# One tile for both halves of the moving operand: modulated activations regrouped into runs of 512 columns

## The chip, the cores and the metric

The kernel runs on one core of a Trainium2 chip, in one launch. The metric is the device time of that launch in microseconds (us), as the median of several runs. A profile is one further execution, recorded by the hardware profiler; its times are read below as us from the start of the recorded span.

## The reference, cut to what matters

The program is two transformer-like blocks over 256 tokens of 1024 features (x), each with a second sequence of 256 tokens (the context). All arithmetic is float32. Each block begins its layers with a normalised and modulated copy of x, and in two places also of the context:

```
h  = rmsnorm(x)   * (1 + scale)   + shift        # x, modulated
hc = rmsnorm(ctx) * (1 + scale_c) + shift_c      # context, modulated
z  = h @ w_in                                    # wide projections, several layers
pc = hc @ w_in[:, some columns]                  # the context needs only a part of them
...
x  = x + gate * swiglu(h2, w_up, w_down)         # feed-forward of the last layer; h2 modulated as above
```

`swiglu` is `(silu(a) * b) @ w_down` with `a, b = split(h2 @ w_up)`; `w_up` is 1024 x 5632 and `w_down` 2816 x 1024.

## The kernel before, in words

Features lie on the 128 partitions, tokens along the free dimension, so an activation of 1024 features is eight feature tiles of 128 x 256 (`KT` = 8, `T` = 256). Weights come from memory in pieces of 1 MB. To keep float32 accuracy with the fast matmul format, every value is split into a high and a low part: ScalarE (ACT) casts the high part, VectorE (DVE) subtracts it to get the low part (`split`, L316 to L318). A product then takes three matmuls into the same bank: high x high, high weight x low activation, low weight x high activation (`mm3`, L364 to L367). The splits of weights run all the time, in quarters of 512 columns, two pieces ahead of use.

The modulated activations live in one tile `HH`, with axes [128, part (high, low), sequence (x, context), 8 feature tiles, 258]. The last two of the 258 columns are used in one trick only (below). So for one feature tile the x columns and the context columns of the same part are each a run of 256, far apart; and so are x's high and low part. Two helpers take both runs in one matmul, as a moving operand of 2 x 256 columns:

- `cols_both` (L381) multiplies a weight column block with x and context at once. It serves the four `xb` pieces of the first layer and the four `f` pieces of the third (`lru_in`, `forget`): 128 such matmuls on each of L365, L366 and L367.
- `cols_split` (L386) serves the feed-forward (all `up` pieces but the first): high weight x (x high, x low) in one matmul of 512 columns (L394), then low weight x (x high) in one of 256 (L395). The two halves of the bank are added by ACT and DVE (L397, L398). It uses two banks in turn, and a bank must be emptied before the next piece may write it.

Everywhere else (`cols2`, `toks`) x alone is used, as runs of 256.

**The early columns.** At the start of the second layer and of the feed-forward, the first weight piece does not wait for the norm. While the residual is added, `residual` (L676 to L681) writes X scaled by `1 + scale`, high and low, into the context half of `HH` (free at that time) and `shift_columns` puts the shift into the two spare columns. `cols_early` (L630) multiplies 48 times with these 258 columns, in the order high weight x high, low weight x high, high weight x low, and then DVE multiplies the two banks with the norm (L643, out `t`), after ACT has copied one column (L642, `c`). Meanwhile ACT computes the norm (`rs`, L300), and `modulate` (L599) makes the proper activations for the later pieces: DVE `xa` (L593), ACT high part (L594), DVE low part (L595), for each of the eight feature tiles.

**What sets the order.** The start of the kernel is written out by hand. From there the tables `L0` to `L3` give the order of steps, and a scheduler places the instructions of each engine by priority and by its own estimate of times; steps in `tc.high_priority()` come first among those that are ready. Each engine executes its list in order, and waits at an instruction whose inputs are not there.

Of the kernel before, what the change touches and what calls it, by code (L numbers as in the profile page):

```python
# [9 lines left out]
F32R = mybir.dt.float32r  # L10
# [13 lines left out]
EARLY = (1, 1)  # L24
# [63 lines left out]
P = 128  # L88
D = 1024
KT = 8  # L90
T = 256
# [136 lines left out]
def build(tc, gates, wp, mp, vec, xT, cT, c2T, tok, cst, crow, out, dbg=None):  # L228
    nc = tc.nc
# [8 lines left out]
    con = pool("con")  # L238
# [7 lines left out]
    def t2(name, shape=(P, 512), dt=F32):  # L246
        return wk.tile(list(shape), dt, name=name, tag="t2", bufs=NT2)

    def t1(name, shape=(P, T), dt=F32):
        return wk.tile(list(shape), dt, name=name, tag="t1", bufs=5)  # L250

    def pair(name, dt=F32):
        return [t4(f"{name}{i}", dt=dt) for i in range(2)]


    HH = con.tile([P, 2, 2, KT, T + 2], F32R, name="hh")

    def h_parts(seq, full=False):
        return [HH[:, i, seq, :, :] if full else HH[:, i, seq, :, 0:T] for i in range(2)]

    def bank(tag, bufs):
        return psum.tile([P, 512], F32, tag=tag, bufs=bufs, name=tag)
# [11 lines left out]
    def v(name, i=0, n=1):  # L274
        o, _ = VOFF[name]
        return V[:, o + i:o + i + n]
# [58 lines left out]
    def load_ahead(n_raw, n_split):  # L335
        while len(raws) < min(npieces, taken[0] + n_raw):
            r = w_p.tile([P, 2048], F32, name="w")
            nc.sync.dma_start(r, wp[len(raws)])
            raws.append(r)
        while len(pieces) < min(npieces, taken[0] + n_split):  # L340
            i = len(pieces)
            pieces.append(halves(raws[i], SW if i > SW_FROM else 2048))
            raws[i] = None
# [8 lines left out]
    def piece(last=False):  # L352

        load_ahead(LR, LSB if last else LS)
        taken[0] += 1
        p = pieces[taken[0] - 1]
        pieces[taken[0] - 1] = None
        return p

    def cut(pc, **kw):  # L360
        (k, n), = kw.items()
        return [w.rearrange(f"p ({k} m) -> p {k} m", **kw) for w in pc]

    def mm3(o, wh, wl, xh, xl, start, stop):  # L364
        nc.tensor.matmul(o, wh, xh, start=start, stop=False)  # L365
        nc.tensor.matmul(o, wh, xl, start=False, stop=False)  # L366
        nc.tensor.matmul(o, wl, xh, start=False, stop=stop)  # L367

    def mm_w(o, w, x, at, start, stop):

        if len(w) == 1:
            nc.tensor.matmul(o, w[0][at], x[0], start=start, stop=stop)
        else:
            mm3(o, w[0][at], w[1][at], x[0], x[1], start, stop)
# [6 lines left out]
    def cols_both(o, w, j):  # L381

        for k in range(KT):
            mm_w(o, w, [HH[:, i, :, k, 0:T] for i in range(2)], np.s_[:, k, 128 * j:128 * (j + 1)], k == 0, k == KT - 1)

    def cols_split(pc, name):  # L386

        w = cut(pc, k=KT)
        o = []
        for j in range(2):  # L390
            b = mm_bank()
            c = np.s_[128 * j:128 * (j + 1)]
            for k in range(KT):
                nc.tensor.matmul(b, w[0][:, k, c], HH[:, :, 0, k, 0:T], start=k == 0, stop=False)  # L394
                nc.tensor.matmul(b[:, 0:T], w[1][:, k, c], HH[:, 0, 0, k, 0:T], start=False, stop=k == KT - 1)  # L395
            o.append(t1(name))
            nc.scalar.copy(o[j], b[:, T:512])  # L397
            nc.vector.tensor_tensor(out=o[j], in0=o[j], in1=b[:, 0:T], op=ALU.add)  # L398
        return o
# [29 lines left out]
    def small(name, n=2):  # L429
        return con.tile([P, n], F32, name=name, tag="small", bufs=4)  # L430
# [145 lines left out]
    def mod_vector(name):  # L576
        while name not in md:
            mod_chunks(1)
        return md[name]

    def scale_g(name, g, sc, i):
        a = con.tile([P, 8], F32, name=name)
        nc.vector.scalar_tensor_tensor(out=a, in0=sc[:, :, i], scalar=1.0, in1=g, op0=ALU.add, op1=ALU.mult)
        return a

    def shift_of(name, sc, i):
        a = con.tile([P, 8], F32, name=name)
        nc.vector.tensor_copy(a, sc[:, :, i])
        return a
# [22 lines left out]
    def sumsq_all(xs):  # L612

        sq = pair("xsq")
        sums = sq[0][:, 2, :]
        for i in range(2):
            nc.scalar.activation(sq[i], xs[i], AF.Square)
        for i in range(2):
            nc.vector.tensor_tensor(out=sq[i][:, 0:2, :], in0=sq[i][:, 0:2, :], in1=sq[i][:, 2:4, :], op=ALU.add)
        nc.vector.tensor_tensor(out=sq[0][:, 0:2, :], in0=sq[0][:, 0:2, :], in1=sq[1][:, 0:2, :], op=ALU.add)  # L620
        nc.vector.tensor_tensor(out=sums, in0=sq[0][:, 0, :], in1=sq[0][:, 1, :], op=ALU.add)
        return token_sums(sums)
# [7 lines left out]
    def cols_early(pc, h, rs):  # L630

        w = cut(pc, k=KT)
        banks = [acc_bank() for j in range(2)]
        for a, b in ((0, 0), (1, 0), (0, 1)):
            for j in range(2):
                for k in range(KT):
                    nc.tensor.matmul(banks[j][:, 0:T + 2], w[a][:, k, 128 * j:128 * (j + 1)], h[b][:, k, :],  # L637
                                     start=k == 0 and a + b == 0, stop=k == KT - 1 and b == 1)
        out = []
        for b in banks:  # L640
            t, c = t1("t"), small("c", 1)
            nc.scalar.copy(c, b[:, T:T + 1])  # L642
            nc.vector.tensor_tensor(out=t, in0=b[:, 0:T], in1=rs, op=ALU.mult)  # L643
            out.append((t, c))
        return out
# [67 lines left out]
    with ExitStack() as st0:  # L713
# [4 lines left out]
        nc.vector.tensor_scalar(out=b1, in0=v("mod_b", 8, 8), scalar1=1.0, scalar2=None, op0=ALU.add)  # L718
        A0 = con.tile([P, 8, 2], F32, name="A0")
        S0 = con.tile([P, 8, 2], F32, name="S0")  # L720
        hx, hc = h_parts(0), h_parts(1)
        acc = [[acc_bank() for i in range(2)] for g in range(2)]
        mod_load(0, nc.sync.dma_start)
        warm_bank[0] = mm_bank()
# [69 lines left out]
        with tc.manual_schedule(engines={mybir.EngineType.PE, mybir.EngineType.DVE, mybir.EngineType.Activation}):  # L794
            for step, s in START:
                if step == "l":
                    for _ in range(s):
                        what, i, j = next(loads)
# [291 lines left out]
                rows += 1  # L1090

        scale1, shift1 = scale_g("a1", v("norm_g", 8, 8), mod_vector("scale1"), 0), shift_of("s1", mod_vector("shift1"), 0)
        early = h_parts(1, True) if EARLY[0] else None
        if early:
            shift_columns(early, shift1)
        table("natural_log_exp_and_others")
# [5 lines left out]

    with ExitStack() as st1:
        lp = st1.enter_context(tc.tile_pool(name="l1", bufs=1))
        hx = h_parts(0)
        with tc.high_priority():
            modulate(lambda k: X[:, k, :], rs1, scale1, shift1, hx)
        mod_chunks(MB[0])
# [72 lines left out]
        def second_context():  # L1181

            c2 = pair("c2")
            for i in range(2):
                nc.gpsimd.dma_start(c2[i], c2T[:, 4 * i:4 * i + 4, :])
            c2k = lambda k: c2[k // 4][:, k % 4, :]
            ms = sumsq_all(c2)
            rsc = rstd_of(ms[:, 0:2], D, 1e-6)
            ac2 = scale_g("ac2", v("g_mix_2", 0, 8), mod_vector("scale2"), 1)
            hc = h_parts(1)  # L1190
            modulate(c2k, rsc, ac2, shift_of("sc2", mod_vector("shift2"), 1), hc)
            return hc

        for name, g, j in L1:
# [8 lines left out]
            elif name == "c2":  # L1203
                hc = second_context()
# [17 lines left out]
        with tc.high_priority():  # L1222
            rs3 = rstd_wide(ms, eps12)
        rs2 = rstd_wide(plain_sums(), eps6)
        hx = h_parts(0)
        with tc.high_priority():
            modulate(lambda k: X[:, k, :], rs3, fgA, shift_of("sx2", mod_vector("shift2"), 0), hx)
        for k in range(KT):
# [5 lines left out]
    with ExitStack() as st2:  # L1234
# [238 lines left out]
        for name, m in L2B:  # L1473
            if name in ("md", "ml"):
                mod_chunks(m, MLATE if name == "ml" else 0)
            elif name == "p":
                w = [p.rearrange("p (w k m) -> p w k m", w=2, k=4) for p in piece()]
                mt = []
                for i, (oh, ol, gate) in enumerate(((oah, oal, "ga"), (obh, obl, "gb"))):
                    b = mm_bank()  # L1480
# [13 lines left out]
        gate2 = con.tile([P, 8], F32, name="gate2h")  # L1494
        nc.vector.tensor_scalar(out=gate2, in0=mod_vector("gate2")[:, :, 0], scalar1=0.5, scalar2=None, op0=ALU.mult)
        scale3, shift3 = scale_g("a4", v("g_ffn_2", 0, 8), mod_vector("scale3"), 0), shift_of("s4", mod_vector("shift3"), 0)
        early = h_parts(1, True) if EARLY[1] else None
        if early:
            shift_columns(early, shift3)
        table("natural_log_exp_and_others")  # L1500
# [2 lines left out]
        with tc.high_priority():  # L1503
            rs4 = rstd_wide(ms, eps6)


    hx = h_parts(0)
    with tc.high_priority():
        modulate(lambda k: X[:, k, :], rs4, scale3, shift3, hx)
    acc = []  # L1510
# [1 line left out]
    for name, m in L3:  # L1512
        if name in ("md", "ml"):
            mod_chunks(m, MLATE if name == "ml" else 0)
        elif name == "up":
            q = m % 2
            if early:
                (sa, ca), (sb, cb) = cols_early(piece(), early, rs4)
                early = None
                act(sa, sa, AF.Silu, bias=ca)  # L1520
                nc.vector.scalar_tensor_tensor(out=sa, in0=sb, scalar=cb, in1=sa, op0=ALU.add, op1=ALU.mult)
            else:
                sa, sb = cols_split(piece(), "sa4")
                act(sa, sa, AF.Silu)
                nc.vector.tensor_tensor(out=sa, in0=sa, in1=sb, op=ALU.mult)
            if q == 0:
                ff[m // 2] = t2("fh", (P, 2, T), F32R), t2("fl", (P, 2, T), F32R)
            split(*(f[:, q, :] for f in ff[m // 2]), sa)
        else:
            fh, fl = ff[m]  # L1530
            if not acc:
                acc.extend(acc_bank() for i in range(4))
            mm_rows(acc, piece(), lambda k: (fh[:, k, :], fl[:, k, :]), m == 0, m == NF // 2 - 1)
# [10 lines left out]
    for m, n in ((0, 1), (1, 1), (2, 2), (4, 2), (6, 2)):  # L1544
        o = X[:, m:m + n, :]
# [23 lines left out]
```

## Time and profile before

| | us |
|---|---|
| median of 3 runs | 924.5 |
| lowest, highest | 923.91, 930.61 |
| the profiled execution | 924.76 |
| its recorded span | 923.0 |

TensorE (PE) is the engine that works through nearly all of the span; DVE and ACT follow with 73% and 58%. Matmuls overlap: the record of one lasts longer than the distance to the next. For the rate of a stretch of matmuls one therefore takes the distance from start to start.

### The profile page before, as it was taken

To read this page: it belongs to the slowest core of one execution; us is meant where nothing else is said; L and a number is where in the kernel's file an instruction comes from. 1 tells how busy PE (TensorE), PEld (TensorE's weight loads), DVE (VectorE), ACT (ScalarE), POOL (GpSimd) and SP (SyncE) were. 2 spreads that over 40 slices of the span, in tenths; PEclk is the share of its full clock that TensorE was granted. 3 is DMA by queue.
4 is the path that set the end of the run, shared out by engine and by line. 5 is a ranking of instruction groups with operands and counts; after the bars stand their busy time and mean duration, and the time that the engine had idled before them with its cause. 6 is when DMAs were issued, how large, how long until landed. Compare 5 with 4: busy or idle time off the path is not lost.

```text
span 923.0 us, 16681 instructions
## 1 busy us (share of the span) xinstructions
PE 897.4 (97%) x6782; PEld 806.8 (87%) x6782; DVE 673.8 (73%) x1283; ACT 539.6 (58%) x985; POOL 15.3 (2%) x27
## 2 busy tenths in 40 slices
PE   8999999899999989999999999999999999999996
PEld 7776787596889789999999898999999999898896
DVE  4578886968766897878874554999688977756644
ACT  3444888686765665547473335972674865645542
POOL 1000000000000000000000000000000000000000
PEclk9999999999999999999999999999999999999999
DMA  9969673254567766664741752355666467555511
GB/s 363 414 221 352 218 251 130 82 176 167 205 251 291 312 233 214 219 238 156 267 137 55 291 202 92 137 184 205 244 218 247 153 216 250 202 184 182 183 46 47
DMA packets 32173, 190.06 MB, mean 206 GB/s; under 512 B 3584, under 2 KB 8064, under 8 KB 10976
## 3 DMA queue, kind: packets, MB, share of 16 engines
q1 hardware_dynamic: 31536, 186.50, 56.7%
q0 software_dynamic: 560, 2.49, 0.7%
q8 instruction: 53, 0.87, 0.4%
q14 instruction: 24, 0.20, 0.1%
HBM read 183.28 MB, written 1.05 MB: 200 GB/s over the span
## 4 chain that ended last, share of the span: by engine, by line
PE 84%; DVE 6%; ACT 6%; DMA 2%; issue 1%; SPq 0%; POOL 0%; DVEq 0%; ACTq 0%; POOLq 0%
PE mm L365 12%; PE mm L367 12%; PE mm L366 12%; PE mm L394 9%; PE acc L366 7%; PE acc L365 7%; PE acc L367 7%; PE mm L395 4%; PE ms L545 2%; PE acc L912 2%; PE acc L790 2%; PE acc L637 1%; DMA w<-in_wp 1%; PE ms L675 1%; ACT L300 1%; ACT w L317 1%
## 5 line engine op out<-in xcount | busy, mean ns | idle before, releaser
L318 DVE TENSOR_TENSOR w<-w 128x512 fp32r<-128x512 f32 x460 | 297.9, 684 | 78.5 <-ACT w L317 74.4
L317 ACT CAST w<-w 128x512 fp32r<-128x512 f32 x460 | 256.0, 618 | 103.1 <-PE mm L366 20.6
L367 PE MATMUL mm<-hh,w 128*128 128x256 f32 (+1 forms) x784 | 237.3, 303 | 2.9 <-DVE w L318 2.9
L365 PE MATMUL mm<-hh,w 128*128 128x256 f32 (+1 forms) x784 | 238.3, 304 | 1.0 <-ACT w L317 1.0
L366 PE MATMUL mm<-hh,w 128*128 128x256 f32 (+1 forms) x784 | 236.0, 301 | 0.0
L365 PEld LDWEIGHTS mm<-hh,w 128*128 128x128 f32 x784 | 148.8, 190 | 14.4 <-issue 5.5
L367 PEld LDWEIGHTS mm<-hh,w 128*128 128x128 f32 x784 | 148.5, 189 | 9.8 <-DVE w L318 3.5
L366 PEld LDWEIGHTS mm<-hh,w 128*128 128x128 f32 x784 | 148.8, 190 | 7.2 <-issue 1.5
L394 PE MATMUL mm<-hh,w 128*128 128x512 f32 x336 | 118.8, 397 | 0.0
L395 PE MATMUL mm<-hh,w 128*128 128x256 f32 x336 | 94.2, 281 | 0.0
L394 PEld LDWEIGHTS mm<-hh,w 128*128 128x128 f32 x336 | 63.2, 188 | 14.7
L504 DVE SCALAR_TENSOR_TENSOR w<-w,crow 128x1024 f32<-128x1024 f32 x40 | 47.7, 1219 | 22.1 <-DMA w<-in_mp 22.0
L395 PEld LDWEIGHTS mm<-hh,w 128*128 128x128 f32 x336 | 63.8, 190 | 0.1
L366 PE MATMUL acc<-fl,w 128*128 128x256 f32 x176 | 49.7, 283 | 0.0
L367 PE MATMUL acc<-fh,w 128*128 128x256 f32 x176 | 49.7, 283 | 0.0
L365 PE MATMUL acc<-fh,w 128*128 128x256 f32 x176 | 49.4, 284 | 0.0
L366 PE MATMUL acc<-yl,w 128*128 128x256 f32 x128 | 37.2, 290 | 0.0
L367 PE MATMUL acc<-yh,w 128*128 128x256 f32 x128 | 36.8, 288 | 0.0
L365 PE MATMUL acc<-yh,w 128*128 128x256 f32 x128 | 36.8, 287 | 0.0
L366 PE MATMUL acc<-zl,w 128*128 128x256 f32 x128 | 36.3, 284 | 0.0
L367 PE MATMUL acc<-zh,w 128*128 128x256 f32 x128 | 36.2, 283 | 0.0
L365 PE MATMUL acc<-zh,w 128*128 128x256 f32 x128 | 36.2, 283 | 0.0
(349 smaller groups left out, 1722.1 us busy)
## 6 DMA issues: line engine op xcount, KB each, us to landing
w<-in_wp SPq DMA_DIRECT2D x115, 1024.0 KB, 5.1
w<-in_mp SPq DMA_DIRECT2D x48, 1024.0 KB, 6.2
four<-up SPq DMA_DIRECT2D x32, 142.0 KB, 4.2
w<-in_wp SPq DMA_DIRECT2D x8, 512.0 KB, 11.3
gw<-in_gates SPq DMA_DIRECT2D x4, 512.0 KB, 4.7
X<-in_xT SPq DMA_DIRECT2D x1, 1024.0 KB, 5.0
ct<-in_cT SPq DMA_DIRECT2D x2, 512.0 KB, 9.7
crow<-in_crow SPq DMA_DIRECT2D x2, 512.0 KB, 13.4
```

What stands on the lines that cost most here:

```text
L300: i = nc.scalar.activation(out, in_, func, **kw).ins
L317: a = nc.scalar.copy(hi, src).ins
L318: return a, nc.vector.tensor_tensor(out=lo, in0=src, in1=hi.bitcast(F32), op=ALU.subtract).ins
L365: nc.tensor.matmul(o, wh, xh, start=start, stop=False)
L366: nc.tensor.matmul(o, wh, xl, start=False, stop=False)
L367: nc.tensor.matmul(o, wl, xh, start=False, stop=stop)
L394: nc.tensor.matmul(b, w[0][:, k, c], HH[:, :, 0, k, 0:T], start=k == 0, stop=False)
L395: nc.tensor.matmul(b[:, 0:T], w[1][:, k, c], HH[:, 0, 0, k, 0:T], start=False, stop=k == KT - 1)
L504: nc.vector.scalar_tensor_tensor(out=w[:, i, :], in0=w[:, i, :], scalar=1.0, in1=s, op0=ALU.mult, op1=ALU.mult, accum_out=o[:, 2 * c + i, :])
L545: nc.tensor.matmul(pm[32 * j:32 * (j + 1), :], s[:, k, :], w[:, 512 * j:512 * (j + 1)], start=c == 0, stop=c == chunks - 1)
L790: nc.tensor.matmul(acc_of(acc[g], i), w[wp_][:, k % 4, 128 * i:128 * (i + 1)], hx[hp][:, k, :], start=k == 0 and i % 2 == 0 and wp_ + hp = ...
L912: nc.tensor.matmul(b[32 * i:32 * (i + 1), 0:T], dg[:, j, i, :], four[:, i, o:o + T], start=j == 0, stop=j == n - 1)
```

## The change

`HH` becomes two tiles, one for the high part (`hh`) and one for the low part (`hl`), each [128, 8 feature tiles, 514]: for a feature tile, 256 columns of x (`LEFT`), then directly 256 of the context (`RIGHT`), then the two spare columns (`MORE` is `RIGHT` and the spare ones). x and context together are now one run of 512 (`BOTH`). In the feed-forward, which has no context, `hh` alone is used: x's high part in `LEFT`, x's low part in `RIGHT`, again one run of 512. Since the early columns of the feed-forward stand in the same `RIGHT` of `hh`, `cols_early` is called before `modulate` there; at the second layer the order of the two calls stays.

```diff
-    HH = con.tile([P, 2, 2, KT, T + 2], F32R, name="hh")
-
-    def h_parts(seq, full=False):
-        return [HH[:, i, seq, :, :] if full else HH[:, i, seq, :, 0:T] for i in range(2)]
+    HH = [con.tile([P, KT, 2 * T + 2], F32R, name=n) for n in ("hh", "hl")]
+    LEFT, RIGHT, BOTH, MORE = slice(0, T), slice(T, 2 * T), slice(0, 2 * T), slice(T, 2 * T + 2)
+
+    def h_parts(where):
+        return [h[:, :, where] for h in HH]
...
-            mm_w(o, w, [HH[:, i, :, k, 0:T] for i in range(2)], np.s_[:, k, 128 * j:128 * (j + 1)], k == 0, k == KT - 1)
+            mm_w(o, w, [h[:, k, BOTH] for h in HH], np.s_[:, k, 128 * j:128 * (j + 1)], k == 0, k == KT - 1)
...
-                nc.tensor.matmul(b, w[0][:, k, c], HH[:, :, 0, k, 0:T], start=k == 0, stop=False)
-                nc.tensor.matmul(b[:, 0:T], w[1][:, k, c], HH[:, 0, 0, k, 0:T], start=False, stop=k == KT - 1)
+                nc.tensor.matmul(b, w[0][:, k, c], HH[0][:, k, BOTH], start=k == 0, stop=False)
+                nc.tensor.matmul(b[:, 0:T], w[1][:, k, c], HH[0][:, k, LEFT], start=False, stop=k == KT - 1)
...
-    hx = h_parts(0)
+    ahead = cols_early(piece(), early, rs4)
+    hx = [HH[0][:, :, LEFT], HH[0][:, :, RIGHT]]
     with tc.high_priority():
         modulate(lambda k: X[:, k, :], rs4, scale3, shift3, hx)
...
-            if early:
-                (sa, ca), (sb, cb) = cols_early(piece(), early, rs4)
-                early = None
+            if ahead:
+                (sa, ca), (sb, cb) = ahead
+                ahead = None
```

The other lines only rename (`h_parts(0)` to `h_parts(LEFT)`, `h_parts(1, True)` to `h_parts(MORE)`). In the built program the order on every engine is the same up to the early columns of the feed-forward. There it moves. Line numbers of the changed kernel are higher by one or two.

DVE at the start of the feed-forward, before, from the low parts of the early columns (`hh<-X`) on; `w<-w` is a quarter of a weight split:

```order
L680 SCALAR_TENSOR_TENSOR hh<-X,a_7764,hh 128x256 x8
L593 SCALAR_TENSOR_TENSOR xa<-X,a_7764,rs 128x256 x4
L595 SCALAR_TENSOR_TENSOR hh<-xa,s_7766,hh 128x256 x4
L593 SCALAR_TENSOR_TENSOR xa<-X,a_7764,rs 128x256 x3
L595 SCALAR_TENSOR_TENSOR hh<-xa,s_7766,hh 128x256 x3
L593 SCALAR_TENSOR_TENSOR xa<-X,a_7764,rs 128x256
L643 TENSOR_TENSOR t<-acc,rs 128x256 x2
L595 SCALAR_TENSOR_TENSOR hh<-xa,s_7766,hh 128x256
```

The same place of the changed kernel, up to the fourth low part; behind it stand three `xa`, three low parts, the last `xa`, the low part `fl` of the feed-forward, a quarter split, and the last low part:

```order
L681 SCALAR_TENSOR_TENSOR hl<-X,a_7765,hh 128x256 x8
L319 TENSOR_TENSOR w<-w 128x512 x5
L644 TENSOR_TENSOR t<-acc,rs 128x256
L319 TENSOR_TENSOR w<-w 128x512 x2
L644 TENSOR_TENSOR t<-acc,rs 128x256
L594 SCALAR_TENSOR_TENSOR xa<-X,a_7765,rs 128x256 x2
L319 TENSOR_TENSOR w<-w 128x512
L596 SCALAR_TENSOR_TENSOR hh<-xa,s_7767,hh 128x256 x2
L594 SCALAR_TENSOR_TENSOR xa<-X,a_7765,rs 128x256 x2
L1523 SCALAR_TENSOR_TENSOR t<-t,c 128x256
L596 SCALAR_TENSOR_TENSOR hh<-xa,s_7767,hh 128x256 x2
```

Eight quarter splits and the two reads of the early banks now stand between the early low parts and the first low part of the modulated x; before, that one stood right behind four `xa`.

ACT at the same place, before, from the last quarter casts ahead of the modulated high parts on (`hh<-xa`):

```order
L317 CAST w<-w 128x512 x2
L594 ACTIVATE hh<-xa,s_7766 128x256 x4
L642 COPY c<-acc 128x1
L594 ACTIVATE hh<-xa,s_7766 128x256 x3
L642 COPY c<-acc 128x1
L594 ACTIVATE hh<-xa,s_7766 128x256
L300 ACT_TABLE_LOAD
L300 ACTIVATE t<-t,c 128x256
```

And of the changed kernel:

```order
L318 CAST w<-w 128x512 x3
L643 COPY c<-acc 128x1
L318 CAST w<-w 128x512 x2
L643 COPY c<-acc 128x1
L301 ACT_TABLE_LOAD
L301 ACTIVATE t<-t,c 128x256
L595 ACTIVATE hh<-xa,s_7767 128x256 x2
L318 CAST w<-w 128x512
L595 ACTIVATE hh<-xa,s_7767 128x256 x2
```

The high parts now stand behind both column copies, the load of the table for silu, and the first silu.

PE behind the 48 early matmuls, in the changed kernel (before, L394 and L395 alternated there from the first feature tile to the last, bank by bank):

```order
L638 MATMUL acc<-hl,w 128x258 x16
L395 MATMUL mm<-hh,w 128x512
L396 MATMUL mm<-hh,w 128x256
L395 MATMUL mm<-hh,w 128x512
L396 MATMUL mm<-hh,w 128x256
L395 MATMUL mm<-hh,w 128x512 x2
L396 MATMUL mm<-hh,w 128x256
L395 MATMUL mm<-hh,w 128x512
L396 MATMUL mm<-hh,w 128x256 x2
```

The scheduler has put matmuls of the second bank between those of the first, so that feature tiles that are there serve both banks while the next ones are awaited. After the last feature tile five matmuls of the piece are left.

## Rows read from the trace of the kernel before

**Rows 1.** The page, part 1: busy us (share of the span) and instructions.

```profile
PE 897.4 (97%) x6782; PEld 806.8 (87%) x6782; DVE 673.8 (73%) x1283; ACT 539.6 (58%) x985; POOL 15.3 (2%) x27
```

**Rows 2.** Windows: length, busy us (instructions) of PE, PEld, DVE, ACT, POOL; clock; DMA.

```profile
480.00:600.00 120.00, 117.28 (x790) 106.89 (x789) 72.34 (x131) 63.75 (x116) 0.00 (x0) 1.00 0.42 150
736.00:912.00 176.00, 176.00 (x1167) 161.50 (x1166) 110.31 (x219) 93.76 (x201) 0.00 (x0) 1.00 0.49 168
```

**Rows 3.** Lines by form, PE: count, busy us, mean ns, idle before.

```profile
L394 PE MATMUL mm<-hh,w 128*128 128x512 f32 x336 | 118.8, 397 | 0.0
...
L365 PE MATMUL mm<-hh,w 128*128 128x512 f32 x128 | 51.0, 398 | 0.0
```

**Rows 4.** Timeline, PE, an f piece (two runs of 256): start us, length us.

```profile
490.81 0.39 PE L365 MATMUL mm<-hh,w 128*128 128x512 f32 x1
...
501.77 0.39 PE L367 MATMUL mm<-hh,w 128*128 128x512 f32 x1
```

**Rows 5.** Timeline, PE, two stretches of recurrent gates (one run of 512).

```profile
102.12 0.40 PE L366 MATMUL acc<-ut,gwh 128*128 128x512 f32 x1
...
103.97 0.39 PE L367 MATMUL acc<-ut,gwl 128*128 128x512 f32 x1
...
109.50 0.39 PE L366 MATMUL acc<-ut,gwh 128*128 128x512 f32 x1
...
111.09 0.39 PE L367 MATMUL acc<-ut,gwl 128*128 128x512 f32 x1
```

**Rows 6.** Timeline, PE, x alone (one run of 256).

```profile
507.68 0.28 PE L365 MATMUL mm<-hh,w 128*128 128x256 f32 x1
...
512.68 0.28 PE L365 MATMUL mm<-hh,w 128*128 128x256 f32 x1
```

**Rows 7.** Timeline, PE, start of the feed-forward: early columns, first and second piece.

```profile
724.12 6.13 PE L637 MATMUL acc<-hh,w 128*128 128x258 f32 x48
730.09 0.39 PE L394 MATMUL mm<-hh,w 128*128 128x512 f32 x1
...
735.72 0.40 PE L394 MATMUL mm<-hh,w 128*128 128x512 f32 x1
```

**Rows 8.** Timeline, DVE, start of the feed-forward.

```profile
725.88 1.66 DVE L593 SCALAR_TENSOR_TENSOR xa<-X,a,rs 128x256 f32<-128x256 f32 x4
727.46 1.66 DVE L595 SCALAR_TENSOR_TENSOR hh<-xa,s,hh 128x256 fp32r<-128x256 f32 x4
...
731.82 0.74 DVE L643 TENSOR_TENSOR t<-acc,rs 128x256 f32<-128x256 f32 x2
...
732.88 1.89 DVE L318 TENSOR_TENSOR w<-w 128x512 fp32r<-128x512 f32 x3
...
735.08 0.41 DVE L398 TENSOR_TENSOR sa<-sa,mm 128x256 f32<-128x256 f32 x1
```

**Rows 9.** Timeline, ACT, start of the feed-forward.

```profile
725.74 1.13 ACT L317 CAST w<-w 128x512 fp32r<-128x512 f32 x2
726.77 1.70 ACT L594 ACTIVATE hh<-xa,s 128x256 fp32r<-128x256 f32 x4
729.32 0.16 ACT L642 COPY c<-acc 128x1 f32<-128x1 f32 x1 [0.84 <-PE acc L637]
...
732.46 1.28 ACT L300 ACT_TABLE_LOAD   x1
...
734.17 0.35 ACT L397 COPY sa<-mm 128x256 f32<-128x256 f32 x1
```

**Rows 10.** Windows and PE timeline around a wait of the second layer.

```profile
327.00:329.00 2.00, 0.38 (x1) 0.19 (x1) 2.00 (x4) 2.00 (x5) 0.00 (x0) 1.00 0.68 160
329.00:331.00 2.00, 0.94 (x4) 0.94 (x5) 2.00 (x5) 2.00 (x5) 0.00 (x0) 0.63 0.86 365
...
330.66 0.41 PE L366 MATMUL mm<-hh,w 128*128 128x256 f32 x1
...
332.37 0.41 PE L365 MATMUL mm<-hh,w 128*128 128x256 f32 x1
```

More of the change, by code (lines that the diff above doesn't have):

```diff
@@ L720, in build @@
         S0 = con.tile([P, 8, 2], F32, name="S0")
-        hx, hc = h_parts(0), h_parts(1)
+        hx, hc = h_parts(LEFT), h_parts(RIGHT)
         acc = [[acc_bank() for i in range(2)] for g in range(2)]
@@ L1092, in build @@
         scale1, shift1 = scale_g("a1", v("norm_g", 8, 8), mod_vector("scale1"), 0), shift_of("s1", mod_vector("shift1"), 0)
-        early = h_parts(1, True) if EARLY[0] else None
+        early = h_parts(MORE) if EARLY[0] else None
         if early:
@@ L1104, in build @@
         lp = st1.enter_context(tc.tile_pool(name="l1", bufs=1))
-        hx = h_parts(0)
+        hx = h_parts(LEFT)
         with tc.high_priority():
@@ L1189, in second_context @@
             ac2 = scale_g("ac2", v("g_mix_2", 0, 8), mod_vector("scale2"), 1)
-            hc = h_parts(1)
+            hc = h_parts(RIGHT)
             modulate(c2k, rsc, ac2, shift_of("sc2", mod_vector("shift2"), 1), hc)
@@ L1224, in build @@
         rs2 = rstd_wide(plain_sums(), eps6)
-        hx = h_parts(0)
+        hx = h_parts(LEFT)
         with tc.high_priority():
@@ L1496, in build @@
         scale3, shift3 = scale_g("a4", v("g_ffn_2", 0, 8), mod_vector("scale3"), 0), shift_of("s4", mod_vector("shift3"), 0)
-        early = h_parts(1, True) if EARLY[1] else None
+        early = h_parts(MORE) if EARLY[1] else None
         if early:
@@ L1504, in build @@
             rs4 = rstd_wide(ms, eps6)
-    hx = h_parts(0)
+    ahead = cols_early(piece(), early, rs4)
+    hx = [HH[0][:, :, LEFT], HH[0][:, :, RIGHT]]
     with tc.high_priority():
```

## The prediction

> **What bounds the kernel now.** I read the page's first part, then windows of the stages that the change touches, then the forms of matmul, then the timeline of single stretches. TensorE (PE) is busy for 97% of the span [rows 1]. That alone could hide waits, since records overlap, so the windows come next: in the 176 us of the feed-forward behind its first piece PE is busy for all of them, and in the 120 us from 480 on, in which the `f` pieces lie, for 117.28 [rows 2]. Neither stage has idle time of PE that could take up a delay, and each nanosecond saved per matmul there is a nanosecond of the kernel.
>
> The change touches 720 matmuls of 512 columns: 336 on L394 and 3 x 128 on L365, L366 and L367 [rows 3]. Their mean length of 397 ns says nothing of their cost; the distance from start to start does. In an `f` piece, with two runs of 256, 47 distances take 501.77 - 490.81 = 10.96 us, **233.2 ns** each [rows 4]. The nearest thing with one run of 512 is the recurrent gates' `ut`: 7 distances take 111.09 - 109.50 = 1.59 us, **227.1 ns** each; another stretch is slower, 8 distances in 103.97 - 102.12 = 1.85 us, 231.3 ns each [rows 5]. One run of 256 takes 5.00 us / 42 = 119.0 ns [rows 6]. [...]
>
> **The gain: one run for two.** 233.2 - 227.1 = 6.1 ns for each of 720 matmuls is 4.4 us. The bounds: with the slower stretch 233.2 - 231.3 = 1.9 ns, 1.4 us. At the other end, a run of 512 may do better in `hh` than in `ut`: doubling the columns in [rows 6] can't cost more than a second 119.0, and of the 227.1 - 119.0 = 108.1 that [rows 5] add, a start-up common to both is part; I allow 7.5 ns, 5.4 us. Below nothing is excluded as far as rows go, since a run of 512 is nowhere slower than two runs there. I take 6.1, from the steadier stretch, whose seven distances are nearly equal.
>
> [...] The rows show a difference of 6.1 ns, and I go by them; zero is a rival.
>
> **The loss: the modulation of the feed-forward comes later.** The early columns now lie where x's low part has to go, so the reads come first, and the built order puts eight quarter splits ahead of the modulation. I follow it on the clock of the trace before. PE's 48 early matmuls start at 724.12 and end at 730.25; at 730.09 the first L394 starts without a gap, and at 735.72 the second piece does, so the first took 5.63 us [rows 7]. Steps: DVE 256 columns (1.58 us for four, start to start) 0.395; read of a bank 0.74 / 2 = 0.37; quarter split 1.89 / 3 = 0.63 [rows 8]. ACT quarter cast 1.13 / 2 = 0.57; high part 0.43; column copy 0.16; table 1.28 [rows 9].
>
> - DVE is through with the early low parts at 725.88 [rows 8]. Five splits end at 729.03. ACT's next cast reuses a buffer of the fifth, so it ends at 729.60, the column copy at 729.76, and DVE's first read of a bank at 730.13.
> - The next split waits for the end of the early matmuls, 730.25. Two splits, to 731.51; second read, 731.88; two `xa`, 732.67; a split, 733.30; the first low part, 733.70. ACT's chain (two casts, copy, table, silu, high part) ends at about 733.2 and just keeps out of the way.
> - So PE starts its first L394 at 733.70 and not at 730.09: **3.6 us idle**.
> - From there to the last low part DVE has 13 more steps of 0.395, `fl` (0.37), a split (0.63) and the last low part (0.40): 740.24. PE uses the feature tiles as they come, on both banks; five matmuls are left, 2 x 233 + 3 x 119 = 0.82 us: 741.06, against 735.72. That is **5.3 us**, the 3.6 among them.
> - The second piece needs the first bank empty: ACT copy 0.35 [rows 9], DVE add 0.41 [rows 8], behind the first bank's last matmul at 740.24 + 0.35 + a length of 0.28: 741.6, another **0.6 us**.
>
> That makes 5.9 us. Nothing behind it gives them back: PE has no idle time later [rows 2]. DVE and ACT lose nothing, as they did their splits first. Of these terms the waits for the engines' signals are left out, and I have rounded splits up; 4.8 to 7.0 are the ends (one step of DVE more or less at each of the three waits).
>
> **The clock.** [...] Matmuls of 256 then came at (332.37 - 330.66) / 8 = 214 ns and not 119, so a dozen of them cost 1.1 us. [...] But PE is waiting for feature tiles through most of 733.7 to 740, and slow matmuls in a wait cost nothing: 0 to 1.7 us, and I take 0.4.
>
> **All else is nothing.** `shift_columns`, the early parts and the modulation are as many instructions with as many elements; the order is the same up to the feed-forward, at the second layer too, where the early columns keep their own space. No DMA is added; SP's and POOL's lists are the same. `HH` shrinks by 32 columns, which only shifts addresses.
>
> **The sum.** 5.9 + 0.4 - 4.4 = +1.9 us. The profiled execution took 924.76, so 926.7; the median before is 0.26 below that execution: **926.4 us**. Gain and loss nearly cancel, and the forecast is no measurable change (under 1%, 9.2 us, is what repeated runs of this kernel, 923.91 to 930.61, can't tell from none).
>
> **The rivals.**
> - [...] 12%.
> - *The stall is smaller.* If DVE's splits are done earlier than I reckon, or PE's wait falls in a place where it waits anyhow, some 2 us of loss with the whole gain: 922. Against it: the order is fixed, and the splits stand ahead. 17%.
> - *Slower.* The clock falls at the first wait and stays low over the broken stretch and on into the next pieces. Each us at the lower level costs half a us once PE has work, and PE has 176 us of it: with no gain (930.8), 6 us at the lower level are 3 us more, 933.8, and from there it is over 1%. [rows 10] show the fall, but full distances again soon after, and the chance that both go wrong is small: 5%.
> - *One run streams without its start-up.* From 119.0 and 227.1, 256 more columns cost 108.1, so 10.9 ns of each matmul aren't columns. Were they gone too, the gain would be 720 x (6.1 + 10.9) = 12.2 us: 918.6. The rows of `ut` are one run already and pay the 10.9. 4%. [...]
>
> **How the numbers follow.** The forecast has the other 62%. Its own range, with gain 1.4 to 5.4, loss 4.8 to 7.0 and clock 0 to 1.7, is 924 to 931 at the likelier ends. With the smaller stall below it and the rival without a gain above it: 921.5 to 931.5, which leaves out the last two rivals and some scatter. Faster by over 1% (under 915.3) needs more than the whole of the last rival: 2%. Slower by over 1% (over 933.7) is the third rival and a bit: 5%. Within 1%: 93%.
>
> **What would show it.** L394 and the 512-column forms of L365 to L367 about 227 ns apart, pairs in the feed-forward 346 and not 352; the early columns of the feed-forward about 2 us earlier than 724.12; PE idle for 3 to 4 us before the first matmul of 512 there, released by DVE's low part, and two or three shorter waits behind; granted clock under 1.00 just there; and from the second piece on the same distance from there to the end, less about 2 us. I am wrong if the distances stay at 233 (then 931), if PE has no idle time at the start of the feed-forward (then 920), or if other stages move.

## The result, and the profile after

| | before | after |
|---|---|---|
| median, us | 925.14 (9 runs) | 933.27 (9 runs) |
| lowest, highest | 923.39, 930.61 | 931.15, 934.86 |
| ratio to before, 95% interval | | 1.0076, 1.0062 to 1.0090 |
| the profiled execution, its span | 924.76, 923.0 | 934.86, 933.1 |

The change makes the kernel 0.76% slower, which is 7.0 us (5.7 to 8.3); the two medians lie 8.1 apart, inside that interval. The forecast was 926.4, within 921.5 to 931.5: the time lies above the range.

**The start of the feed-forward.** Before the change PE has no wait there (none between 720 and 745). The waits of PE in the changed kernel (us in total, times, longest) now have this at their head, and a second one at L395 (which was L394):

```profile
PE mm L395 <- DVE hh L596: 3.6, 1, 3.6
...
PE mm L395 <- DVE sa L399: 0.5, 1, 0.5
```

PE's timeline shows where they lie: early columns, first matmul of 512, last of the first piece, second piece.

```profile
728.12 4.16 PE L638 MATMUL acc<-hh,w 128*128 128x258 f32 x32
732.12 2.09 PE L638 MATMUL acc<-hl,w 128*128 128x258 f32 x16
737.84 0.76 PE L395 MATMUL mm<-hh,w 128*128 128x512 f32 x1 [3.63 <-DVE hh L596]
...
745.08 0.28 PE L396 MATMUL mm<-hh,w 128*128 128x256 f32 x1
745.86 0.50 PE L395 MATMUL mm<-hh,w 128*128 128x512 f32 x1 [0.50 <-DVE sa L399]
```

Against the first early matmul, the first L394 came at 730.09 - 724.12 = 5.97 us and the second piece at 735.72 - 724.12 = 11.60 [rows 7]; now 737.84 - 728.12 = 9.72 and 745.86 - 728.12 = 17.74. So the start of PE's new work is 3.75 us late and the second piece **6.14 us late**. DVE's timeline tells why:

```profile
729.87 3.27 DVE L319 TENSOR_TENSOR w<-w 128x512 fp32r<-128x512 f32 x5
733.89 0.42 DVE L644 TENSOR_TENSOR t<-acc,rs 128x256 f32<-128x256 f32 x1 [0.74 <-ACT c L643]
734.25 1.29 DVE L319 TENSOR_TENSOR w<-w 128x512 fp32r<-128x512 f32 x2
735.46 0.42 DVE L644 TENSOR_TENSOR t<-acc,rs 128x256 f32<-128x256 f32 x1
735.79 0.87 DVE L594 SCALAR_TENSOR_TENSOR xa<-X,a,rs 128x256 f32<-128x256 f32 x2
736.58 0.68 DVE L319 TENSOR_TENSOR w<-w 128x512 fp32r<-128x512 f32 x1
737.21 0.89 DVE L596 SCALAR_TENSOR_TENSOR hh<-xa,s,hh 128x256 fp32r<-128x256 f32 x2
...
743.70 0.48 DVE L596 SCALAR_TENSOR_TENSOR hh<-xa,s,hh 128x256 fp32r<-128x256 f32 x1
```

Where four `xa` and a low part stood before [rows 8], DVE now does five splits, a read, two splits, a read, two `xa`, a split, and only then the first low part. The first low part starts 9.09 us behind the first early matmul (it was 727.46 - 724.12 = 3.34), the last one 15.58. The windows there (length; busy us of PE, PEld, DVE, ACT, POOL; granted clock; DMA) show a granted clock of 0.50 when PE starts again, and of 1.00 from 742 on:

```profile
736.00:738.00 2.00, 0.16 (x1) 0.19 (x2) 2.00 (x5) 1.99 (x5) 0.00 (x0) 0.96 0.17 70
738.00:740.00 2.00, 2.00 (x6) 1.46 (x7) 2.00 (x7) 1.28 (x4) 0.00 (x0) 0.50 0.03 8
740.00:742.00 2.00, 2.00 (x9) 1.73 (x10) 2.00 (x7) 1.31 (x3) 0.00 (x0) 0.69 0.00 0
742.00:744.00 2.00, 2.00 (x13) 1.77 (x12) 2.00 (x6) 0.51 (x1) 0.00 (x0) 1.00 0.00 0
```

**The distances.** Timeline of PE after: 47 distances of an `f` piece, then four whole `up` pieces of the feed-forward (64 pairs of L395 and L396).

```profile
495.03 0.40 PE L366 MATMUL mm<-hh,w 128*128 128x512 f32 x1
...
505.91 0.39 PE L368 MATMUL mm<-hh,w 128*128 128x512 f32 x1
...
791.51 0.40 PE L395 MATMUL mm<-hh,w 128*128 128x512 f32 x1
...
814.17 0.40 PE L395 MATMUL mm<-hh,w 128*128 128x512 f32 x1
```

The same four pieces before:

```profile
781.22 0.40 PE L394 MATMUL mm<-hh,w 128*128 128x512 f32 x1
...
803.80 0.40 PE L394 MATMUL mm<-hh,w 128*128 128x512 f32 x1
```

In the `f` piece (505.91 - 495.03) / 47 = 231.5 ns against 233.2 [rows 4]; in the feed-forward (814.17 - 791.51) / 64 = 354.1 a pair against 22.58 / 64 = 352.8. Over all undisturbed distances of the two traces (no wait and no other work between the two starts) the means are 231.5 against 233.5 (374 distances each) and 353.5 against 352.9 (318 and 327 pairs). So 384 matmuls gain 2.0 ns, 0.8 us, and 336 lose 0.6 ns, 0.2 us: a gain of **0.6 us, where 4.4 were forecast**. Whether the 2.0 ns belong to the one run or to its new place in memory, no run here separates. From the second piece to the end of the span the two traces take the same time, 923.0 - 735.72 = 187.3 us before and 933.1 - 745.86 = 187.2 after.

**What is not the change.** The early columns of this execution start 4.0 us later than before (728.12 against 724.12), which would add two thirds to the loss if it belonged to the change. Matched one by one, the matmuls of after are 1.3 us behind those of before 20 us into the span, another 1.7 us behind the wait at 176, and another 1.3 us behind two waits around 330. Behind the first the granted clock fell in after (0.51 in 178 to 180) and not in before (1.00); around 330 it fell in both, and stayed low longer in after (0.50 to 0.66 in the windows from 331 to 339) than in before (0.63 and 0.52 in those from 329 to 333). Windows of after, of before, and of an experiment that has before's layout (`order_only`, below):

```profile
178.00:180.00 2.00, 2.00 (x3) 0.68 (x2) 2.00 (x5) 0.59 (x1) 0.77 (x2) 0.51 0.86 361
...
333.00:335.00 2.00, 2.00 (x11) 2.00 (x11) 2.00 (x5) 1.22 (x3) 0.00 (x0) 0.50 0.23 90
```

```profile
178.00:180.00 2.00, 2.00 (x6) 0.76 (x4) 2.00 (x4) 1.66 (x3) 0.00 (x0) 1.00 0.37 152
```

```profile
178.00:180.00 2.00, 2.00 (x4) 0.97 (x3) 2.00 (x4) 0.69 (x1) 0.08 (x1) 0.50 0.49 201
...
333.00:335.00 2.00, 2.00 (x20) 2.00 (x19) 2.00 (x5) 0.46 (x1) 0.00 (x0) 1.00 0.34 57
...
732.00:734.00 2.00, 0.00 (x0) 0.00 (x0) 2.00 (x6) 1.99 (x4) 0.00 (x0) 0.77 0.53 221
734.00:736.00 2.00, 1.52 (x5) 1.37 (x5) 2.00 (x6) 1.56 (x5) 0.00 (x0) 0.50 0.03 8
...
738.00:740.00 2.00, 2.00 (x8) 1.71 (x7) 2.00 (x6) 0.93 (x3) 0.00 (x0) 0.53 0.00 0
```

At 178 the profiled execution of before kept a clock of 1.00; of all 14 executions with a profile four did and ten didn't (0.50 to 0.56 in the lower of the windows 177 to 179 and 179 to 181), each group with both layouts in it, and the fall cost 1.5 to 1.7 us. At 333 the loss was 0 to 2.7 us from one execution to the next, again in both layouts (in `order_only` and `early_apart` the clock was 1.00 in all windows from 325 to 341). The start varied too: 20 us into the span `order_only` was level with before, and an experiment with the new layout (`early_apart`, below) 1.0 us behind. One profile against another can therefore mislead by 4 us here, and the profiled execution of the changed kernel is the slowest of its nine; the verdicts below rest on repeated runs, the stages on distances within one stage.

### The profile page after: what moved, and what is told of

It reads as the page before. It is cut to its first block, busy times and chain, and to the rows that moved or that the text cites. A ratio compares the mean times of both kernels' runs of the same rounds, so it can differ in the third digit from the quotient of the medians.

```text
span 933.1 us, 16680 instructions
## 1 busy us (share of the span) xinstructions
PE 903.2 (97%) x6782; PEld 810.8 (87%) x6782; DVE 674.3 (72%) x1283; ACT 540.2 (58%) x985; POOL 15.3 (2%) x27
## 4 chain that ended last, share of the span: by engine, by line
PE 84%; DVE 7%; ACT 6%; DMA 1%; issue 1%; POOL 0%; SPq 0%; DVEq 0%; ACTq 0%; POOLq 0%
PE mm L366 12%; PE mm L368 12%; PE mm L367 11%; PE mm L395 9%; PE acc L366 7%; PE acc L367 7%; PE acc L368 7%; PE mm L396 4%; PE ms L546 2%; PE acc L913 2%; PE acc L791 2%; PE acc L638 1%; PE ms L676 1%; ACT L301 1%; DVE w L319 1%; ACT w L318 1%
## 5 line engine op out<-in xcount | busy, mean ns | idle before, releaser
L368 PE MATMUL mm<-hh,w 128*128 128x256 f32 (+1 forms) x784 | 237.7, 303 | 2.8 <-DVE w L319 2.8
L366 PE MATMUL mm<-hh,w 128*128 128x256 f32 (+1 forms) x784 | 239.0, 305 | 1.0 <-ACT w L318 1.0
L367 PE MATMUL mm<-hl,w 128*128 128x256 f32 (+1 forms) x784 | 236.5, 302 | 0.0
L366 PEld LDWEIGHTS mm<-hh,w 128*128 128x128 f32 x784 | 149.2, 190 | 14.1 <-issue 5.5
L368 PEld LDWEIGHTS mm<-hh,w 128*128 128x128 f32 x784 | 149.3, 190 | 9.5 <-DVE w L319 3.4
L367 PEld LDWEIGHTS mm<-hl,w 128*128 128x128 f32 x784 | 149.3, 190 | 6.9 <-issue 1.5
L395 PE MATMUL mm<-hh,w 128*128 128x512 f32 x336 | 120.6, 401 | 4.1 <-DVE hh L596 3.6
L396 PE MATMUL mm<-hh,w 128*128 128x256 f32 x336 | 94.9, 284 | 0.0
L395 PEld LDWEIGHTS mm<-hh,w 128*128 128x128 f32 x336 | 64.1, 191 | 19.5 <-issue 3.8
L396 PEld LDWEIGHTS mm<-hh,w 128*128 128x128 f32 x336 | 64.3, 191 | 0.2
```

Source lines behind the costliest of these rows:

```text
L395: nc.tensor.matmul(b, w[0][:, k, c], HH[0][:, k, BOTH], start=k == 0, stop=False)
L396: nc.tensor.matmul(b[:, 0:T], w[1][:, k, c], HH[0][:, k, LEFT], start=False, stop=k == KT - 1)
```

## The experiments

Theory A: the order costs it all, and runs of 512 in `hh` are hardly faster than two of 256. Theory B: the new layout itself is dearer. The first four ran on one chip, beside 29 runs of before (median 926.53).

**The order alone.** Layout of before; the call is moved.

```diff
+    ahead = cols_early(piece(), early, rs4)
     hx = h_parts(0)
     with tc.high_priority():
         modulate(lambda k: X[:, k, :], rs4, scale3, shift3, hx)
...
-                (sa, ca), (sb, cb) = cols_early(piece(), early, rs4)
+                (sa, ca), (sb, cb) = ahead
```

> The layout of before, with the early matmuls of the feed-forward called ahead of its modulation: the order on every engine is that of the changed kernel. Theory A (the order costs it all, the runs of 512 give nothing): PE idle 3.6 us before the first L394, the piece behind it broken, clock at half for some 3 us; +6 us, 931. Theory B (the new layout itself is dearer, by addresses or by the second tile): the order costs under 2 us, 925 to 927, since the matmuls of the first feed-forward piece could then use what was idle. The prediction's sum (order +6.3) says 931.4.

Measured: 933.30 (6 runs), ratio 1.0081 (1.0063 to 1.0099). PE's timeline, then the last low part in DVE's:

```profile
724.75 6.13 PE L637 MATMUL acc<-hh,w 128*128 128x258 f32 x48
734.48 0.77 PE L394 MATMUL mm<-hh,w 128*128 128x512 f32 x1 [3.60 <-DVE hh L595]
...
743.41 0.50 PE L394 MATMUL mm<-hh,w 128*128 128x512 f32 x1 [0.51 <-DVE sa L398]
```

```profile
740.34 0.48 DVE L595 SCALAR_TENSOR_TENSOR hh<-xa,s,hh 128x256 fp32r<-128x256 f32 x1
```

The same idle time with the same releaser, and the same ratio as the whole change, without its layout. Theory B falls. The second piece comes 743.41 - 724.75 = 18.66 us behind the first early matmul, 7.06 later than before and 0.92 later than in the changed kernel. DVE is not the reason for the 0.92: its last low part starts 740.34 - 724.75 = 15.59 us behind the first early matmul, against 15.58 there. What differs in the rows is PE's granted clock: here it is 0.50 to 0.77 in the windows from 732 to 740 (the last ones above), in the changed kernel 0.50 and 0.69 in those from 738 to 742.

**The layout alone.** The feed-forward's early columns go into the low tile, which the feed-forward doesn't use; the order is that of before (`cols_early` stands behind `modulate` again). From here on the edits are shown against the changed kernel.

```diff
-    HH = [con.tile([P, KT, 2 * T + 2], F32R, name=n) for n in ("hh", "hl")]
+    HH = [con.tile([P, KT, 516], F32R, name=n) for n in ("hh", "hl")]
...
-        early = h_parts(MORE) if EARLY[1] else None
+        early = [HH[1][:, :, 0:T + 2], HH[1][:, :, 258:258 + T + 2]] if EARLY[1] else None
```

> The new layout, with the feed-forward's early columns in the low tile, which is free there (516 wide), so that the modulation need not wait; the order on every engine is that of before. Theory A: no idle PE at the start of the feed-forward; 720 runs of 512 are worth 0 to 1 us, so 924 to 925. The prediction's gain of 6.1 ns a matmul says 920.7. Theory B (layout dearer): 930 or more.

Measured: 924.91 (12 runs), ratio 0.9987 (0.9971 to 1.0004). No PE wait is left at the start of the feed-forward, and the second piece comes 735.89 - 724.30 = 11.59 us behind the first early matmul, as in before (11.60). PE's timeline, with four `up` pieces at its end:

```profile
724.30 6.06 PE L638 MATMUL acc<-hl,w 128*128 128x258 f32 x48
...
735.89 0.40 PE L395 MATMUL mm<-hh,w 128*128 128x512 f32 x1
...
781.37 0.39 PE L395 MATMUL mm<-hh,w 128*128 128x512 f32 x1
...
803.94 0.40 PE L395 MATMUL mm<-hh,w 128*128 128x512 f32 x1
```

22.57 / 64 = 352.7 a pair, so nothing gained there; the 512-column matmuls of x and context come at 231.4 on the mean. By these distances the layout is worth 0.8 us, within theory A's 0 to 1; by the runs it is 1.2 us faster (2.7 faster to 0.4 slower). The prediction's 4.4 lies outside both.

**Two runs again.** The same kernel, x's low part two columns further on.

```diff
-    hx = [HH[0][:, :, LEFT], HH[0][:, :, RIGHT]]
+    hx = [HH[0][:, :, LEFT], HH[0][:, :, T + 2:2 * T + 2]]
...
-                nc.tensor.matmul(b, w[0][:, k, c], HH[0][:, k, BOTH], start=k == 0, stop=False)
+                nc.tensor.matmul(b, w[0][:, k, c], HH[0][:, k, :].rearrange("p (s t) -> p s t", s=2)[:, :, 0:T], start=k == 0, stop=False)
```

> The same as the kernel with the early columns apart, but x's low part lies two columns further, so the 336 matmuls of 512 columns in the feed-forward read two runs of 256 again. If the number of runs has a price of 6 ns, this is 2.0 us slower than that kernel and L394/L395 pairs are 6 ns longer; if it has none, the two differ by under 0.5 us and pairs stay at 353 ns.

Measured: 926.74 (11 runs), ratio 1.0000 (0.9986 to 1.0014). The same four pieces:

```profile
783.13 0.39 PE L395 MATMUL mm<-hh,w 128*128 128x512 f32 x1
...
805.76 0.40 PE L395 MATMUL mm<-hh,w 128*128 128x512 f32 x1
```

22.63 / 64 = 353.6. With order and tiles equal, the mean of all pairs rises by 0.8 ns (353.5 against 352.7), 0.3 us in the feed-forward, and not by 6.1. In single feature tiles the difference is anything from -7.6 to +7.7 ns, and the low part also lies two columns further on, so what of the 0.8 is the second run's and what the place's stays open. The medians differ by 1.8 us, but the intervals overlap, and of the 1.9 us between the two profiled executions 1.7 are there before the feed-forward's early columns start.

**Places in memory.** If not the number of runs, what makes a run in `hh` dearer than the 227 ns of `ut`? First, every feature tile of the high tile to a multiple of 64 bytes (528 columns).

> The same as the kernel with the early columns apart, but a feature tile of the high tile has 528 columns and not 516, so every run starts at a multiple of 64 bytes. Theory C (a run of 512 takes 233 and not 227 ns because its feature tiles start at odd multiples of 16 bytes): L394 and the high x parts of the 512-column matmuls fall to 227 ns, pairs from 353 to 347 ns; 336 x 6 + 256 x 5 = 3.3 us, 921. If addresses do nothing: 353 and 924.5.

Measured: 923.84 (11 runs), ratio **0.9975 (0.9962 to 0.9989)**, faster than both kernels. Four pieces:

```profile
782.35 0.40 PE L395 MATMUL mm<-hh,w 128*128 128x512 f32 x1
...
804.75 0.40 PE L395 MATMUL mm<-hh,w 128*128 128x512 f32 x1
```

22.40 / 64 = 350.0 a pair: 2.7 of the 6 ns that theory C asked for (350.2 on the mean of all pairs). The distances behind L395 (medians over 42 column blocks) are 235, 235, 230, 230, 235, 235, 230, 230 ns for feature tiles 0 to 7, nearly the same in every piece; the other 512-column matmuls come at 232.5 and don't gain. So I let the moving operand, the weights, or both always be those of one feature tile (which leaves part of the product out):

```diff
-                nc.tensor.matmul(b, w[0][:, k, c], HH[0][:, k, BOTH], start=k == 0, stop=False)
-                nc.tensor.matmul(b[:, 0:T], w[1][:, k, c], HH[0][:, k, LEFT], start=False, stop=k == KT - 1)
+                nc.tensor.matmul(b, w[0][:, k, c], HH[0][:, 0, BOTH], start=k == 0, stop=False)
+                nc.tensor.matmul(b[:, 0:T], w[1][:, k, c], HH[0][:, 0, LEFT], start=False, stop=k == KT - 1)
```

> The kernel with the early columns apart and aligned, but every matmul of the feed-forward's split pieces reads feature tile 0 instead of its own (that part of the computation is left out). Theory C2 (where the moving columns lie makes a run of 512 dearer than 227 ns): the distance of all eight L395 of a piece becomes one number, 227 or 235, and pairs fall to 347 or stay at one level. Theory E (the weights' places, or weight and moving read together): the pattern over k stays, 235, 235, 230, 230. Theory F (512 after 256 costs a switch, whatever the places): 350 to 353 a pair in all three of these kernels.

> The same with feature tile 2 (2112 x 2 bytes further). Theory C2: one number again, and another than with tile 0, 230 against 235. Theory E and F: as with tile 0.

> The same base, every matmul of these pieces reads the weights of feature tile 0 and its own moving tile (the rest of the weights is left out). Theory C2: the pattern over k stays, 235, 235, 230, 230. Theory E: one number for all k, 227 to 235. Theory F: pairs at 350 to 353.

> The same base, both fixed to tile 0. Theories C2 and E: one number for all k, and if places are the whole cause some 347 ns a pair (2 us less in the feed-forward than 350); theory F: 350 to 353 a pair.

Moving tile 0 always, then tile 2 always, then the weights of tile 0 always, four pieces each:

```profile
782.06 0.40 PE L395 MATMUL mm<-hh,w 128*128 128x512 f32 x1
...
804.67 0.40 PE L395 MATMUL mm<-hh,w 128*128 128x512 f32 x1
```

```profile
780.12 0.39 PE L395 MATMUL mm<-hh,w 128*128 128x512 f32 x1
...
802.55 0.39 PE L395 MATMUL mm<-hh,w 128*128 128x512 f32 x1
```

```profile
782.02 0.40 PE L395 MATMUL mm<-hh,w 128*128 128x512 f32 x1
...
804.42 0.40 PE L395 MATMUL mm<-hh,w 128*128 128x512 f32 x1
```

On the means of all pairs: 353.4 with tile 0, 350.0 with tile 2 (350.8 with seven pairs of 388 to 397 ns counted in), and 350.3 with the pattern 235, 235, 230, 230 kept within 1 ns where the weights are fixed; both fixed to tile 0, 353.3. So which moving tile is read moves the mean by 3 ns, and the place of the weights doesn't. My expectation of one number for all k failed: with the moving tile fixed at 0 two values still alternate (medians 238 and 232), with the weights fixed too, and no run shows why. Theory F, a price of the change from 512 to 256, is not excluded: no kernel's mean came under 349.0. Single feature tiles did, with 346 ns in the last kernel below, which is no more than 227.1 + 119.0. Which property of a place counts? All tiles 32 bytes further on, and the two tiles 11776 bytes further on:

> The kernel with the early columns apart and aligned, with all its tiles 32 bytes further on: every run of the high tile starts 32 bytes behind a multiple of 64, as the tiles do whose matmuls come at an even 120 and 227 ns (ut, and the mixed products' dh). Theory C3 (that place within 64 bytes decides): pairs fall from 350 to 347 ns, 1 us less, about 922.9 beside 923.8. If it doesn't: 350 to 353 and no difference.

> The same base, the high and low tile 11776 bytes further on, behind the vectors and x, at the same place within 256 bytes as in the aligned kernel. Theory G (the tiles' place in the memory as a whole, at its low end, makes their runs dearer): pairs fall towards 347. If only the place within 256 bytes counts: 350 and the pattern 235, 235, 230, 230 over the feature tiles.

The 32 bytes change next to nothing: 350.7 a pair, the same pattern within 2 ns, ratio 0.9992 (0.9981 to 1.0004). Theory C3 falls. The tiles moved far, same place within 256 bytes:

```profile
782.67 0.40 PE L396 MATMUL mm<-hh,w 128*128 128x512 f32 x1
...
805.02 0.39 PE L396 MATMUL mm<-hh,w 128*128 128x512 f32 x1
```

22.35 / 64 = 349.2, the pattern is another (228, 230, 232, 232 from tile 0 on), and the matmuls of x and context fall from 232.5 to 231.2. The same kernel, timed:

> The kernel with the early columns apart and aligned, its two tiles 11776 bytes further on, timed. Its profile showed 349.0 ns a pair where the aligned one has 350.2, and 231.2 ns for the 512-column matmuls of x and context where that has 232.5: 336 x 1.1 + 384 x 1.3 = 0.9 us less than the aligned kernel, 3.2 us less than before. If places that far away do nothing for the whole, 0.9975 of before again.

923.84 (12 runs), ratio 0.9981 (0.9964 to 0.9997): no better than the aligned one as far as runs can tell; the 0.9 us that its distances promised is inside the interval. A second profile of this kernel gave the same mean a pair as the first, 349.1 and 349.0.

**Where the loss comes from.** The changed kernel, early columns in their shared place, the 48 matmuls still ahead; only the reads of their banks go behind the modulation. `early_read` is the part of `cols_early` that reads the banks.

```diff
-    ahead = cols_early(piece(), early, rs4)
+    ahead = cols_early(piece(), early)            # the 48 matmuls alone
...
-                (sa, ca), (sb, cb) = ahead
+                (sa, ca), (sb, cb) = early_read(ahead, rs4)
```

> The changed kernel with its layout, the early columns where they are, and the 48 early matmuls still ahead of the modulation in the program; only the two reads of their banks (ACT's column copies, DVE's products with the norm) stand behind the modulation again. Theory A1 (the loss comes from the bank reads and the quarter splits that go ahead of the modulation with them, not from the shared place): the first low part waits only for the 32 matmuls that read the high early columns, 4.0 us after the first of them; the last one is some 1.2 us late, so 925.5 to 926.5 where before takes 925.1. Theory A2 (the shared place forces the loss): 931 to 933.

Measured: 925.73 (12 runs; before on that chip 925.64), ratio 0.9993 (0.9976 to 1.0010). DVE's timeline, then PE's:

```profile
725.93 0.69 DVE L319 TENSOR_TENSOR w<-w 128x512 fp32r<-128x512 f32 x1
726.54 1.67 DVE L596 SCALAR_TENSOR_TENSOR hh<-xa,s,hh 128x256 fp32r<-128x256 f32 x4
```

```profile
722.59 4.16 PE L638 MATMUL acc<-hh,w 128*128 128x258 f32 x32
726.59 2.09 PE L638 MATMUL acc<-hl,w 128*128 128x258 f32 x16
728.52 0.40 PE L395 MATMUL mm<-hh,w 128*128 128x512 f32 x1
...
734.63 0.50 PE L395 MATMUL mm<-hh,w 128*128 128x512 f32 x1 [0.20 <-DVE sa L399]
```

The first low part starts at 726.54, as PE goes over to the early low columns. That is 3.95 us behind the first early matmul and not 3.34: the shared place holds it up by 0.61 us, in which DVE does one split. The second piece is 734.63 - 722.59 = 12.04 us behind the first early matmul, 0.44 later than before. Theory A1 holds, and the loss is smaller than the 1.2 us I had allowed: of the 6.1 us, **5.7 came from the bank reads, with the splits and the table load that went ahead with them, and 0.4 from the shared place.**

## Why the prediction was wrong

- **The loss was right.** Forecast: first matmul of 512 3.6 us late with DVE's low part as releaser, first piece 5.3 us late, another 0.6 for the bank, 5.9 in all. Measured: 3.63 idle, 0.50 at the bank, 6.14 in all; without the change's layout 7.06. That is no luck of the total: the sum over DVE's new list had the end of the last low part at 740.24, 16.12 us behind the first early matmul, and it came 743.70 + 0.48 - 728.12 = 16.06 behind it. Of the "two or three shorter waits behind" only the one at the bank shows.
- **The clock** fell where forecast: to 0.50 in 738 to 740 in the changed kernel, and in 734 to 736 in the kernel with the order alone. Its term of 0.4 was my estimate, and no run shows it by itself; what the runs show in its place is the rest of the loss, 0.2 in the changed kernel (6.14 - 5.9) and 1.2 in the kernel with the order alone (7.06 - 5.9), where the clock stayed low longer.
- **The step that failed is the gain**, "233.2 - 227.1 = 6.1 ns for each of 720 matmuls": 4.4 us forecast, 0.6 measured. I took 227.1 from seven distances because they were nearly equal. All 43 distances of `ut` in the trace before have a mean of 228.6, and even that would have given 4.9 ns and 3.5 us; `hh` as one run came to 231.5 in `cols_both`, and that the slower stretch of [rows 5], 231.3, is so near is luck, as the other places gave 231.2 to 232.5. A difference between two tiles was read as a difference between one run and two; with tiles and order held equal the second run, with its shift of two columns, adds 0.8 ns. My bound below, "a run of 512 is nowhere slower than two runs there", was wrong too: as one run, pairs came out 0.6 ns dearer.
- **The rival that came true** is the one without a gain: the loss in full, 924.5 + 6.3 = 930.8, to which I gave 12%. The runs show for it the 0.8 ns between one run and two at equal order and tiles, and the 3.4 ns between two feature tiles (353.4 and 350.0) that are both one run; why places differ, no run shows. The rival "slower" names 933.8, near the 933.27, but by a clock that stays low into the next pieces; it was back at 1.00 by 742, before the second piece at 745.86.
- **The sum** with the measured terms: 6.1 to 7.1 for the start of the feed-forward, less 0.6, is 5.5 to 6.5 us, of which all but the lowest part lies inside the 5.7 to 8.3 of the runs. The 0.5 to 1.5 us that the middle of the runs, 7.0, has beyond it are inside the interval, and stay unexplained.
- **The base** was the median of three runs, 924.5; that of nine is 925.14. Of the 1.8 us by which the time passed the range, 0.6 lie there.
- **The range** was too short above. It ended at 931.5, below the 924.5 + 7.0 + 1.7 - 1.4 = 931.8 of its own ends and 0.7 above the rival's 930.8, though the loss alone had ends 2.2 us apart and the clock 1.7. With no gain, a loss of 7.0 and a clock of 1.7 it would have had to reach 933.2.
- "Early columns 2 us earlier" failed: they came 4.0 later, three quarters of it by the clock at 178 and 333, the rest in the first 20 us; the 0.8 us gained in the `xb` and `f` pieces is hidden in it.

## What to carry to other kernels

When an edit frees or shares a buffer, list what the scheduler now puts ahead of the critical producer: the shared place cost 0.4 us, and the bank reads called before the producer, with their companions, 5.7. A difference of some nanoseconds between two matmul streams is not a price of their shape until places are held equal; the mean over all of them is safer than the steadiest few, but here it would have misled too. Give the matmuls first and their evacuation last when the same engine also feeds the next matmuls.

## What the runs showed of the hardware

- The fast matmul format: in the trace of before, matmuls of 512 columns in fp32r (`ut`) come 227 ns apart on the median, those on unsplit float32 (`u`, L372) 429 ns.
- The distance of matmuls of 512 columns in fp32r depends on where the moving columns lie: 350.0 or 353.4 ns a pair for two feature tiles of one tile, 349.0 to 353.5 on the means of the kernels run, where two profiles of one layout agree within 0.2 ns. A shift of 32 bytes moved the mean by 0.5 ns and fixing the weights by 0.1; how busy DVE, ACT or the DMA engines are shows no effect (sorted by the busy share of each, fifths of the pairs of before average 352.2 to 353.7 ns). Which bits of the place count stays open.
- `dh`, `fh`, `mh` and `zh`, in other tiles, come at 120 ns a matmul of 256 in the traces of before and after (119.9 and 120.0 on the mean), where those of the modulated activations vary by feature tile, with medians from 114 to 127 and a mean of 118.7 and 119.1.
- PE's wait at 176 is 2.4 us in before, 2.5 in after and 2.4 in `order_only`; behind it the granted clock stayed at 1.00 in four of the 14 executions with a profile, before among them, and fell to 0.50 to 0.56 in ten. Behind the two waits around 330 (1.7 and 1.0 us in before, 1.6 and 1.0 in after, 1.7 and 1.0 in `order_only`) it fell to 0.52 in before and 0.50 in after and stayed at 1.00 in `order_only`; the lower clock cost 0 to 2.7 us there. Together with the 1.5 to 1.7 at 176 that is up to 4.4 us, about half of the spread of all runs of before, 922.75 to 931.86.
